# The head of a hybrid decoder step: new order of squares, normalizing products, masks and gate products

## The chip, the cores and the metric

The kernel runs on one core of a Trainium2 chip. The metric is device time in microseconds (us) for one launch; the median of the runs is compared. The core has a matrix engine (PE, which multiplies out of the on-chip memory into accumulation banks), a vector engine (DVE), an activation engine (ACT), a general engine (POOL) and a queue (SP) that issues nearly all transfers. Each engine runs its own instructions strictly in the order of its queue; semaphores order them between engines.

## The reference

One layer of a hybrid decoder on 512 prompt tokens and 8 x 8 sample tokens (576 columns in all), model width 1024:

```python
u = rmsnorm(h, norm_mix);  proj = u @ w_in            # z, xbc, dt | r, k, v, w_lo, a_lo, g_lo
prev = concat([shift_state, rw])[:, :-1]
u = rw + (prev - rw) * shift_mu                       # token shift, RWKV-7 part
w = -softplus(-(w0 + tanh(w_lo) @ w2)) - 0.5
a = sigmoid(a0 + a_lo @ a2)
gate = sigmoid(g_lo) @ g2                             # g_lo: 128 columns
# RWKV-7 recurrence, per-head group norm, bonus, output gate
# Mamba-2 SSD on conv(xbc), silu(z) gate, grouped RMSNorm
h += concat([y_ssd, y_rwkv]) @ w_out
h += swiglu(rmsnorm(h));  h += sigmoid(rmsnorm(h) @ w_plg) * (p @ w_plp);  y = rmsnorm(h)
```

Beside y the final and new states are returned.

## The kernel before

Everything is kept transposed: 128 channels on the partitions, 576 tokens along the free dimension. An input of 1024 channels is eight tiles x0 to x7. Products run in three passes, so that two reduced-precision halves stand for one full-precision number: a raw weight block (four 128x128 blocks, 256 KB) is loaded by SP, ACT rounds it to a high half `whi`, and POOL or DVE subtracts to get the low half `wlo` (`wsplit`, L197; the engine alternates through `flip` unless `only[0]` names one). `wload` (L211) takes a block that was loaded early from the list `ahead`, if there is one. Two blocks make a projected tile; `mm3` (L219) issues high x high, high x low, low x high in two column halves, 48 matrix products a tile. The result goes to one of two `lin` banks (`lin_ps`, L107).

The head, in the order of the code:

- Constants and masks (L120 to L179): `ones`, `blk`, `ident` and the masks are written by POOL; `dgmask` is multiplied by `dmb` on DVE (L164 to L167).
- The shift states `sst` are loaded (L263), then a weight block, then x0 to x7 with a second block behind x3 (L290 to L298).
- Per x tile, ACT makes the high half of x times the norm weight (L303) and DVE the low half (L304): `XU`, the input without its token-wise norm factor.
- Per x tile the square, by ACT (POOL for x3), and running sums on DVE (L307 to L317); the square tiles have four buffers in two pairs. `rstd_by_token` sums over channels on PE (L332), takes the root on ACT (L336) and the reciprocal on DVE (L337), and transposes it to all partitions (L340); ACT copies it to `r0` (L345, L346).
- `shifted` (L356) projects a tile and applies the token shift. With `early` it multiplies `XU` and scales the result by `r0` afterwards (`u`, L361), which frees the bank. ACT starts the shifted tile (L366), DVE finishes it with three operations (L368, L369, L371), ACT saves two pieces for the output.
- `norm_x` (L350) makes the normalized x on DVE (L352) and splits it in a high half (ACT) and a low half (`split`, L194; POOL and DVE in turn).
- LORA (L428) is the first projected tile, with a tanh and a split; then `norm_x(3)`, GATE (`gate_in`, L432), `norm_x(5)`.
- Then the four quarters (L926). Quarter 0 takes two of its six tiles, then the eight gate products (`gates`, L439: two weight blocks, eight times six matrix products, ACT copies each result, SP writes it out), then the other four tiles (`fill_for`). Below they are called t0 to t5, all `early`. `prep`, `gram`, `solve`, `chain` and `head_norm` follow per quarter, with further projected tiles as fillers between them.

The order of instructions in each engine's queue is not that of the code: a planner simulates the program and hands out what is ready, with the order of the code as priority. `tc.issue_after(ins)` ties the instructions of its block that run on the engine of `ins` behind `ins` in that queue.

Of the kernel before, what the change touches and what calls it, by code (L numbers as in the profile page):

```python
# [8 lines left out]
F32 = mybir.dt.float32  # L9
F32R = mybir.dt.float32r  # L10
AF = mybir.ActivationFunctionType
# [5 lines left out]
P = 128  # L17
D = 1024
NT = 576
# [56 lines left out]
def hybrid_step(ctx, tc, A):  # L76
# [15 lines left out]
    def act(out, in_, func=AF.Copy, scale=1.0, bias=0.0):  # L92
        return S.activation(out, in_, func, bias=bias, scale=scale)  # L93
# [13 lines left out]
    def lin_ps(off=224):  # L107
        return lin_bank()[:, off:off + NT]
# [19 lines left out]
    def par(name, i=0):  # L128
        at, _ = PV[name]
        return pv[:, at + i:at + i + 1]  # L130
# [30 lines left out]
    for h in range(2):  # L161
        keep(dmb[h * 64:h * 64 + 64, :], [[-8, 8]], 0, 1)
        keep(dmb[h * 64:h * 64 + 64, :], [[8, 8]], 7, -1)
    for i in range(2):  # L164
        V.tensor_tensor(dgmask[:, i, :].rearrange("p (b t) -> p b t", b=8),
                        dgmask[:, i, :].rearrange("p (b t) -> p b t", b=8),
                        dmb[:].unsqueeze(2).to_broadcast([P, 8, 8]), ALU.mult)  # L167
    hw = const("hw", [P, 76])
    at, _ = PV["w0"]
    V.tensor_scalar(hw[:, 0:16], pv[:, at:at + 16], 0.5, None, ALU.mult)  # L170
# [40 lines left out]
    def wload(nk, hi=None, lo=None):  # L211
        if ahead:
            return ahead.pop(0)
        n = nk * P
        src = A["wts"][wat[0]:wat[0] + P * n].rearrange("(p n) -> p n", p=P)
        wat[0] += P * n
        return wsplit(src, n, hi, lo)
# [42 lines left out]
    G.memset(rmask[:, 128:NT:64], 0.0)  # L260

    sst = se.tile([P, 26, 9], F32, tag="sst", name="sst")
    nc.sync.dma_start(sst[:], A["s_shift"])  # L263
    sho = se.tile([P, 26, 9], F32, tag="sho", name="sho")

    def cx_ps():
# [21 lines left out]


    xr = []  # L290
    early_w = [wload(4)]
    for k in range(KT):
        x = slot("x")
        nc.sync.dma_start(x[:], A["xT"][k])
        xr.append(x)
        if k == 3:
            early_w.append(wload(4))
    ahead += early_w  # L298
    xu = [(se, sp)[i].tile([P, KT, NT], F32R, tag=f"G{i}", name=nm("xu")) for i in range(2)]
    XU = []  # L300
    for k in range(KT):
        hi, lo = xu[0][:, k], xu[1][:, k]
        act(hi, xr[k][:], AF.Identity, scale=par("norm_mix", k))  # L303
        V.scalar_tensor_tensor(lo, xr[k][:], par("norm_mix", k), hi.bitcast(F32), ALU.mult, ALU.subtract)  # L304
        XU.append((hi, lo))
    accs = {}
    for k in range(KT):  # L307
        sq = (se, sp)[k % 2].tile([P, NT], F32, tag=f"bk{k % 2}", name=nm("sq"), bufs=2)
        e = G if k in SQP else V
        if e is G:  # L310
            G.tensor_tensor(sq[:], xr[k][:], xr[k][:], ALU.mult)
        else:
            act(sq[:], xr[k][:], AF.Square)
        if e in accs:
            e.tensor_tensor(sq[:], sq[:], accs[e][:], ALU.add)
        accs[e] = sq
    V.tensor_tensor(accs[V][:], accs[V][:], accs[G][:], ALU.add)  # L317
    r0 = sp.tile([P, NT], F32, tag="gt", name=nm("rstd"), bufs=2)
# [26 lines left out]
    act(r0[:, 0:448], banks[0][:, 0:448])  # L345
    act(r0[:, 448:NT], banks[1][:, 0:128])  # L346

    X = []

    def norm_x(n):  # L350
        for k in range(len(X), len(X) + n):
            V.scalar_tensor_tensor(xr[k][:], xr[k][:], par("norm_mix", k), r0[:], ALU.mult, ALU.mult)  # L352
            X.append(split(xr[k][:], xp, ("xhi", "xlo"), [P, NT]))


    def shifted(c, early=False, odd=False):  # L356
        ps = lin_ps()
        if early:
            linear(XU, ps)
            u = se.tile([P, NT], F32, tag="ar", name=nm("u"), bufs=2)  # L360
            V.tensor_tensor(u[:], ps, r0[:], ALU.mult)  # L361
            ps = u[:]
        else:
            linear(X, ps)
        t = sp.tile([P, NT], F32, tag="vo", name=nm("rw"), bufs=2) if odd else slot("rw")
        act(t[:], ps, AF.Identity, scale=omu[:, c:c + 1])  # L366
        mu = par("shift_mu", c)
        V.scalar_tensor_tensor(t[:, 0:65:8], sst[:, c, :], mu, t[:, 0:65:8], ALU.mult, ALU.add)  # L368
        V.scalar_tensor_tensor(t[:, ND + 1:NT], ps[:, ND:NT - 1], mu, t[:, ND + 1:NT], ALU.mult, ALU.add)  # L369
        t8, p8 = (a[:, 0:ND].rearrange("p (b t) -> p b t", b=8) for a in (t, ps))  # L370
        V.scalar_tensor_tensor(t8[:, :, 1:8], p8[:, :, 0:7], mu, t8[:, :, 1:8], ALU.mult, ALU.add)  # L371
        act(sho[:, c, 0:8], ps[:, 7:64:8])
        act(sho[:, c, 8:9], ps[:, NT - 1:NT])
        return t
# [72 lines left out]

    norm_x(3)
    ugh = gate_in()
    norm_x(5)  # L450


    H = (slice(0, 64), slice(64, 128))
# [17 lines left out]
    def fill(n=1):  # L471

        for _ in range(min(n, len(todo))):
            which, c = todo.pop(0)
            if which == "xbc":
                conved(c)
            elif which == "z":
                zed(c)
            elif which == "dt":
                dts()  # L480
            else:
                Q[which].t.append(shifted(c, which == 0, which % 2 and len(Q[which].t) > 3))
# [442 lines left out]

    for s in Q:  # L926
        if s.q == 0:
            fill(2)
            gates(ugh)
        fill_for(s)  # L930
        prep(s)
        start_states(s)
        gram(s)
        bonus(s)
        decayed(s)
        if s.q < 3:
            inverse(s)
            chain(s)
            head_norm(s)
# [733 lines left out]
```

## Time and profile before

| | us |
|---|---|
| median of 3 runs | 1346.01 |
| lowest, highest run | 1341.81, 1350.75 |
| span of the profiled execution, first to last instruction | 1349.0 |

The profiled execution has no time of its own beside its span; the span lies 3.0 us above the median of the three runs and inside their spread. An instruction's row in the order of time reads: start, duration, engine, line, operation, output<-inputs, shapes, and in brackets how long the engine had been idle before it and which instruction ended the wait. L93 is the helper through which all ACT operations go, so they are told apart by the names of their tiles. A line with a count merges neighbours.

### The profile page before, as it was taken

The numbers are of one execution on the slowest core, as the hardware profiler recorded it, in microseconds if no ns is written. First come the engines' busy times: TensorE is split into PE (matmuls) and PEld (weight loads), VectorE is DVE, ScalarE is ACT, GpSimd is POOL, SyncE is SP. The second block draws the span as 40 slices with busy tenths as digits, with TensorE's granted clock in tenths as the row PEclk, the third lists the DMA queues.
The fourth block names the chain that finished last, engine by engine and source line by source line (L and its number), as shares of the span: only waits on it lengthen the run. The fifth ranks groups of instructions, "written<-read, shape, count | busy, mean of one in ns | idle before, by whom it ended". The sixth has DMA issues, their size and how long they took to land.

```text
span 1349.0 us, 26596 instructions
## 1 busy us (share of the span) xinstructions
PE 1246.8 (92%) x10525; PEld 1150.7 (85%) x10525; DVE 826.0 (61%) x1443; ACT 618.9 (46%) x1256; POOL 625.6 (46%) x597
## 2 busy tenths in 40 slices
PE   6897999999989978899999969989999999999997
PEld 6787897889868957788779859889999999999997
DVE  6648666887687785943466667886553135443454
ACT  6565436534654463343434364464442124433363
POOL 5425413642355154122456645565654336654642
PEclk9897799899979978889989989998999999999998
DMA  5322242234232412262454542222323222314322
GB/s 164 125 68 66 77 117 63 85 103 116 75 99 78 109 41 80 94 214 83 157 176 131 179 125 72 73 93 88 92 88 87 79 86 82 93 59 149 96 89 71
DMA packets 94461, 135.58 MB, mean 100 GB/s; under 512 B 34705, under 2 KB 39057, under 8 KB 94337
## 3 DMA queue, kind: packets, MB, share of 16 engines
q1 hardware_dynamic: 93760, 133.36, 32.4%
q8 instruction: 83, 1.36, 0.4%
q10 hardware_dynamic: 576, 0.52, 0.1%
q14 instruction: 42, 0.34, 0.1%
HBM read 106.10 MB, written 27.75 MB: 99 GB/s over the span
## 4 chain that ended last, share of the span: by engine, by line
PE 63%; DVE 14%; ACT 4%; issue 4%; DMA 3%; POOL 3%; DVEq 0%; SPq 0%; ACTq 0%; POOLq 0%
PE lin L234 21%; PE lin L1403 8%; PE lin L223 6%; PE lin L221 6%; PE lin L222 6%; DVE h L395 2%; PE lin L1508 1%; PE lin L1509 1%; PE lin L1510 1%; DVE tmp L674 1%; DVE wlo L206 1%; DVE Tt L676 1%; PE lin L613 1%; PE cx L797 1%; DVE suv L831 1%
## 5 line engine op out<-in xcount | busy, mean ns | idle before, releaser
L206 POOL TENSOR_TENSOR wlo<-raw,whi 128x512 fp32r<-128x512 f32 (+1 forms) x108 | 146.4, 1356 | 352.5 <-ACT whi L93 269.5
L93 ACT ACTIVATE whi<-raw 128x512 fp32r<-128x512 f32 (+1 forms) x232 | 143.3, 618 | 259.1 <-PE lin L234 126.4
L221 PE MATMUL lin<-xhi,whi 128*128 128x288 f32 (+1 forms) x784 | 243.3, 311 | 2.5 <-ACT whi L93 2.2
L223 PE MATMUL lin<-xhi,wlo 128*128 128x288 f32 (+1 forms) x784 | 241.5, 308 | 2.3 <-POOL wlo L206 2.3
L222 PE MATMUL lin<-xlo,whi 128*128 128x288 f32 (+1 forms) x784 | 241.5, 308 | 0.3 <-POOL xlo L194 0.3
L206 DVE TENSOR_TENSOR wlo<-raw,whi 128x512 fp32r<-128x512 f32 (+1 forms) x124 | 100.9, 814 | 103.2 <-PE lin L234 60.4
L221 PEld LDWEIGHTS lin<-xhi,whi 128*128 128x128 f32 (+1 forms) x784 | 151.0, 193 | 9.3 <-ACT whi L93 2.6
L223 PEld LDWEIGHTS lin<-xhi,wlo 128*128 128x128 f32 (+1 forms) x784 | 150.7, 192 | 6.2 <-POOL wlo L206 2.8
L222 PEld LDWEIGHTS lin<-xlo,whi 128*128 128x128 f32 (+1 forms) x784 | 150.8, 192 | 4.8 <-issue 1.2
L234 PE MATMUL lin<-xhi,whi 128*128 128x288 f32 x384 | 62.3, 297 | 3.2 <-ACT xhi L93 3.0
L234 PE MATMUL lin<-xlo,whi 128*128 128x288 f32 x384 | 60.8, 298 | 0.0
L234 PE MATMUL lin<-xhi,wlo 128*128 128x288 f32 x384 | 59.3, 297 | 0.0
L234 PEld LDWEIGHTS lin<-xhi,whi 128*128 128x128 f32 x384 | 54.6, 189 | 3.8 <-ACT xhi L93 1.7
L234 PEld LDWEIGHTS lin<-xlo,whi 128*128 128x128 f32 x384 | 54.8, 191 | 0.0
L234 PE MATMUL lin<-ah,wlo 128*128 128x288 f32 x352 | 54.7, 296 | 0.0
L234 PE MATMUL lin<-al,whi 128*128 128x288 f32 x352 | 54.7, 296 | 0.0
L234 PE MATMUL lin<-ah,whi 128*128 128x288 f32 x352 | 54.7, 296 | 0.0
L234 PEld LDWEIGHTS lin<-xhi,wlo 128*128 128x128 f32 x384 | 54.3, 191 | 0.0
L1403 PE MATMUL lin<-T,wh 128*128 128x288 f32 x320 | 50.1, 296 | 4.5 <-DVE T L194 2.8
L674 DVE TENSOR_TENSOR tmp<-L,Tt 72x30 f32<-72x30 f32 (+14 forms) x120 | 49.2, 410 | 3.2
L234 PEld LDWEIGHTS lin<-ah,whi 128*128 128x128 f32 x352 | 49.6, 189 | 0.0
L234 PEld LDWEIGHTS lin<-ah,wlo 128*128 128x128 f32 x352 | 49.6, 189 | 0.0
(425 smaller groups left out, 3197.8 us busy)
## 6 DMA issues: line engine op xcount, KB each, us to landing
raw<-wts SPq DMA_DIRECT2D x271, 256.0 KB, 2.6
S<-s_wkv SPq DMA_DIRECT2D x8, 512.0 KB, 5.1
hd<-s_ssm SPq DMA_DIRECT2D x8, 512.0 KB, 4.5
o_ssm_s<-hd SPq DMA_DIRECT2D x8, 512.0 KB, 2.9
xbc_d<-E SPq DMA_DIRECT2D x12, 288.0 KB, 2.1
x<-xT SPq DMA_DIRECT2D x8, 288.0 KB
gate_d<-g SPq DMA_DIRECT2D x8, 288.0 KB, 2.5
bv_d<-rw SPq DMA_DIRECT2D x8, 288.0 KB
```

What stands on the lines that cost most here:

```text
L93: return S.activation(out, in_, func, bias=bias, scale=scale)
L206: eng.tensor_tensor(lo[:, 0:n], raw[:, 0:n], hi[:, 0:n].bitcast(F32), ALU.subtract)
L221: T.matmul(ps[:, a:b], whi, xhi[:, a:b], start=first, stop=False)
L222: T.matmul(ps[:, a:b], whi, xlo[:, a:b], start=False, stop=False)
L223: T.matmul(ps[:, a:b], wlo, xhi[:, a:b], start=False, stop=last)
L234: T.matmul(ps[:, a:e], (hi, lo)[p][:, i * P:(i + 1) * P], xs[k + i][q][:, a:e], start=n == k + i == 0, stop=n == 2 and k + i == nk - 1, sk ...
L395: V.scalar_tensor_tensor(h[:], E[:, i:i + 600], w(i), h[:], ALU.mult, ALU.add)
L613: T.matmul(ps[:, c:c + 128].rearrange("p (a t) -> p a t", a=2), s.BK[jj][H[e], g].rearrange("p a t -> p (a t)"), s.G[H[e], g, jj, :, e], s ...
L674: V.tensor_tensor(o, L[:, jx:jx + 1, jx + 1:32].to_broadcast([NB, jx, n]), Tt[:, 0:jx, jx:jx + 1].to_broadcast([NB, jx, n]), ALU.mult)
L676: V.tensor_tensor(Tt[:, 0:jx, jx + 1:32], Tt[:, 0:jx, jx + 1:32], o, ALU.subtract)
L797: T.matmul(uw[H[e], jj, :], TT[H[e], g, jj, :], xs[H[e], jj, :], start=True, stop=True)
L1403: T.matmul(ps, (hi, lo)[p][:, k * P:(k + 1) * P], OPS[n][k][q], start=first and p == q == k == 0, stop=p == 1 and k == 3, skip_group_check ...
```

## The change

Seven edits, all in the head:

1. Ten full-precision products of `ones` with itself go into a `lin` bank ahead of the first weight block. Nothing reads the bank.
2. The low half of the first weight block goes to DVE; from then on all low halves of weights go to POOL, until quarter 0 has four tiles.
3. The load of the shift states moves from ahead of the first weight block to behind x5.
4. On ACT all squares, and on DVE all their sums, are tied behind the conversions of x7.
5. The mask products on DVE move from the constants to behind the last low half of x.
6. `norm_x` is tied behind the last operation of the latest token shift on DVE, its low halves all go to DVE, and after GATE only one x tile is normalized; the other four follow one by one behind t0 to t3.
7. The gate products come after four tiles of quarter 0, not two.

```diff
-    for i in range(2):
-        V.tensor_tensor(dgmask[:, i, :].rearrange("p (b t) -> p b t", b=8),
-                        dgmask[:, i, :].rearrange("p (b t) -> p b t", b=8),
-                        dmb[:].unsqueeze(2).to_broadcast([P, 8, 8]), ALU.mult)
...
-    nc.sync.dma_start(sst[:], A["s_shift"])
...
+    t = lin_ps()
+    for _ in range(10):
+        T.matmul(t[:, 0:P], ones[:], ones[:], start=True, stop=True)
+    only[0] = V
     early_w = [wload(4)]
+    only[0] = G
     for k in range(KT):
...
+        if k == 5:
+            nc.sync.dma_start(sst[:], A["s_shift"])
...
-        act(hi, xr[k][:], AF.Identity, scale=par("norm_mix", k))
-        V.scalar_tensor_tensor(lo, xr[k][:], par("norm_mix", k), hi.bitcast(F32), ALU.mult, ALU.subtract)
+        last = (act(hi, xr[k][:], AF.Identity, scale=par("norm_mix", k)),
+                V.scalar_tensor_tensor(lo, xr[k][:], par("norm_mix", k), hi.bitcast(F32), ALU.mult, ALU.subtract))
         XU.append((hi, lo))
+    with tc.issue_after(last[1].ins):
+        for i in range(2):
+            V.tensor_tensor(dgmask[:, i, :].rearrange("p (b t) -> p b t", b=8),
+                            dgmask[:, i, :].rearrange("p (b t) -> p b t", b=8),
+                            dmb[:].unsqueeze(2).to_broadcast([P, 8, 8]), ALU.mult)
...
-            act(sq[:], xr[k][:], AF.Square)
+            with tc.issue_after(last[0].ins):
+                act(sq[:], xr[k][:], AF.Square)
         if e in accs:
-            e.tensor_tensor(sq[:], sq[:], accs[e][:], ALU.add)
+            with tc.issue_after(last[1].ins) if e is V else nullcontext():
+                e.tensor_tensor(sq[:], sq[:], accs[e][:], ALU.add)
...
-    X = []
+    X, shifts = [], []
     def norm_x(n):
         for k in range(len(X), len(X) + n):
+          with tc.issue_after(shifts[-1].ins):
             V.scalar_tensor_tensor(xr[k][:], xr[k][:], par("norm_mix", k), r0[:], ALU.mult, ALU.mult)
-            X.append(split(xr[k][:], xp, ("xhi", "xlo"), [P, NT]))
+            X.append(split(xr[k][:], xp, ("xhi", "xlo"), [P, NT], lo_eng=V))
...
-        V.scalar_tensor_tensor(t8[:, :, 1:8], p8[:, :, 0:7], mu, t8[:, :, 1:8], ALU.mult, ALU.add)
+        shifts.append(V.scalar_tensor_tensor(t8[:, :, 1:8], p8[:, :, 0:7], mu, t8[:, :, 1:8], ALU.mult, ALU.add))
...
     norm_x(3)
     ugh = gate_in()
-    norm_x(5)
+    norm_x(1)
...
         if s.q == 0:
-            fill(2)
+            for _ in range(4):
+                fill()
+                norm_x(1)
+            only[0] = None
             gates(ugh)
         fill_for(s)
```

## The prediction

> **What bounds the kernel now.** I read the page first, then the waits of PE alone in the first 90 us, then the order of PE, DVE, ACT and POOL there. The whole program is PE's:
>
> ```profile
> span 1349.0 us, 26596 instructions
> PE 1246.8 (92%) x10525; PEld 1150.7 (85%) x10525; DVE 826.0 (61%) x1443; ACT 618.9 (46%) x1256; POOL 625.6 (46%) x597
> ```
>
> PE is idle for 8% of the span, so time comes back only where PE stands still or runs at a lower clock. The change touches the head: two projected tiles (LORA, GATE), then quarter 0's six tiles t0 to t5 and eight gate products. PE's waits there:
>
> ```profile
> PE lin L221 <- ACT xu L93: 6.6, 1, 6.6
> PE lin L223 <- DVE wlo L206: 5.4, 1, 5.4
> PE lin L223 <- POOL wlo L206: 2.1, 1, 2.1
> PE lin L221 <- DVE u L361: 1.6, 1, 1.6
> ```
>
> The columns are total, times, longest, in us. 6.6 is the wait for the first input; 5.4 is a wait in t1 for a low weight half that stood in DVE's queue; 1.6 is t0 waiting for a bank that `u` has to empty, which needs the norm factor r0. PE in order of time, and under it one row of the table by stretches (its last three figures are granted clock, DMA share, GB/s):
>
> ```profile
> 27.80 0.71 PE L340 MATMUL cx<-ident,rn 128*128 128x128 f32 x5
> 30.09 0.38 PE L221 MATMUL lin<-xu,whi 128*128 128x288 f32 x1 [1.57 <-DVE u L361]
> 40.20 0.30 PE L222 MATMUL lin<-xu,whi 128*128 128x288 f32 x1
> 45.93 0.61 PE L223 MATMUL lin<-xu,wlo 128*128 128x288 f32 x1 [5.44 <-DVE wlo L206]
> 46.34 0.45 PE L221 MATMUL lin<-xu,whi 128*128 128x288 f32 x1
> 46.58 0.45 PE L222 MATMUL lin<-xu,whi 128*128 128x288 f32 x1
> 50.41 0.30 PE L223 MATMUL lin<-xu,wlo 128*128 128x288 f32 x1
> 50.95 0.29 PE L221 MATMUL lin<-vo,whi 128*128 128x288 f32 x1
> 59.31 0.30 PE L221 MATMUL lin<-xu,whi 128*128 128x288 f32 x1
> ...
> 45.00:50.00 5.00, 4.07 (x17) 4.07 (x18) 5.00 (x8) 2.13 (x5) 3.92 (x2) 0.50 0.21 59
> ```
>
> Starts are 0.24 us apart after the 5.44 us wait (46.34 to 46.58), at a granted clock of 0.50, until 50.41: the wait cost its length and then half the clock for 4 us. And DVE:
>
> ```profile
> 22.29 0.76 DVE L317 TENSOR_TENSOR sq<-sq,sq 128x576 f32<-128x576 f32 x1
> 26.11 0.19 DVE L337 RECIPROCAL rn<-rn 128x5 f32<-128x5 f32 x1 [2.46 <-ACT rn L93]
> 29.19 0.76 DVE L361 TENSOR_TENSOR u<-lin,rstd 128x576 f32<-128x576 f32 x1
> 32.72 6.68 DVE L352 SCALAR_TENSOR_TENSOR x<-x,pv,rstd 128x576 f32<-128x576 f32 x5
> 39.46 1.96 DVE L369 SCALAR_TENSOR_TENSOR rw<-u,pv,rw 128x511 f32<-128x511 f32 x1
> 43.02 0.74 DVE L369 SCALAR_TENSOR_TENSOR rw<-u,pv,rw 128x511 f32<-128x511 f32 x1
> 45.20 0.68 DVE L206 TENSOR_TENSOR wlo<-raw,whi 128x512 fp32r<-128x512 f32 x1
> 78.65 0.76 DVE L361 TENSOR_TENSOR u<-lin,rstd 128x576 f32<-128x576 f32 x1 [3.65 <-PE lin L223]
> 85.04 0.76 DVE L361 TENSOR_TENSOR u<-lin,rstd 128x576 f32<-128x576 f32 x1 [3.69 <-PE lin L223]
> ```
>
> Five normalizing products hold DVE for 6.68 us ahead of LORA's shift, and the weight half at 45.20 comes after all of it. The last two rows close t4 and t5, and DVE had been idle for over 3.6 us before each: a tile on a free PE is 85.04 - 78.65 = 6.39 us, or 0.133 for each of its 48 products.
>
> **The change part by part.** Two points frame the sum: the start of t0 (30.09) and the end of t5 (`u` at 85.04), 54.95 us apart.
>
> *From t0 to t5.* Six tiles are 6 x 6.39 = 38.3 us, the gate products 59.31 - 50.95 = 8.4 us, together 46.7. The other 8.3 us are the 5.44 us wait, the slow clock behind it and smaller waits. The change takes their cause away: only one normalizing product stays between GATE and t0, four stand behind the shifts of t0 to t3, and each sits behind the latest shift in DVE's queue; the low weight halves all go to POOL until the fourth tile. So I credit 8.3. The debit is POOL, now alone with the halves:
>
> ```profile
> 39.29 0.62 ACT L93 ACTIVATE whi<-raw 128x512 fp32r<-128x512 f32 x1
> 44.46 2.70 POOL L194 TENSOR_TENSOR ull<-rw,ulh 128x576 fp32r<-128x576 f32 x1 [3.58 <-ACT ulh L93]
> 63.32 1.29 POOL L206 TENSOR_TENSOR wlo<-raw,whi 128x512 fp32r<-128x512 f32 x1 [5.95 <-ACT whi L93]
> 39.46 1.42 POOL L194 TENSOR_TENSOR xlo<-x,xhi 128x576 fp32r<-128x576 f32 x1 [1.41 <-ACT xhi L93]
> ```
>
> A half tile of weights lasts PE 6.39 / 2 = 3.2 us; its conversion takes 0.62 on ACT and 1.29 on POOL, so 1.3 us are spare. The split of LORA (2.70) stands in the same queue: 2.70 - 1.3 = 1.4 us late, once. I take 1.5 us; the ends are 0 and another 5.4. The low halves of x move from POOL to DVE: three more operations of about 0.76 us, beside tiles in which DVE idles for 3.6 us and more; nothing, and if that cover failed, `u` has a spare tile time, since a second bank is filling. The gate products wait for the same ACT copies as now; behind t3 their input is old, which is worth some tenths, taken as 0.
>
> *Up to t0.* r0 needs the squares of all eight x tiles. ACT and the transfers:
>
> ```profile
> 5.00:10.00 5.00, 1.21 (x2) 0.57 (x2) 2.87 (x9) 4.53 (x8) 4.62 (x16) 1.00 1.00 345
> 5.80 0.78 ACT L93 ACTIVATE xu<-x,pv 128x576 fp32r<-128x576 f32 x1 [0.27 <-DMA x<-xT]
> 20.71 0.69 ACT L93 ACTIVATE sq<-x 128x576 f32<-128x576 f32 x1 [3.35 <-DVE sq L315]
> 24.51 1.28 ACT L93 ACT_TABLE_LOAD   x1
> 25.81 0.27 ACT L93 ACTIVATE rn<-cx,eps_t 128x5 f32<-128x5 f32 x1
> x<-xT SPq DMA_DIRECT2D x8, 288.0 KB
> 12.81 1.31 DVE L165 TENSOR_TENSOR dgmask<-dgmask,dmb 128x64 bf16<-128x64 bf16 x2
> ```
>
> Estimate from these rows: the first x is there at 5.8; seven more of 0.295 MB and a weight block of 0.262 MB at 345 GB/s take 6.7 us, so the last lands at 12.5. In the queue of transfers, the one of the shift states goes past a weight block and six x; the bytes ahead of the last x stay, so it lands when it did, and the first shift needs the states only after r0. The last conversion ends at 12.5 + 0.78 = 13.3, and now all squares start there: two are done at 13.3 + 2 x 0.69 = 14.7. The mask products (1.31), now behind the last low half (13.3 + 0.76 = 14.1), hold DVE to 15.4. The buffers make the rest serial, as the 3.35 us wait of a square on DVE shows: five sums at 0.76 to 19.2, a square of 0.69 to 19.9, two sums to 21.4. Before it was 22.29 + 0.76 = 23.05: 1.65 gained. GATE's weight conversions stand behind such waiting squares on ACT; a square waits for two sums, 1.5 us, about what a half tile spares (1.3), so they cost 0.2, inside GATE, whose end does not set t0.
>
> The column sums that follow:
>
> ```profile
> 24.10 0.75 PE L332 MATMUL cx<-ones,sq 128*64 128x1 f32 x20
> ```
>
> From there to `u` it took 29.19 - 23.05 = 6.1 us. Of these the column sums waited for PE to 24.10, the root for a table load (24.51 + 1.28), the transposes until 27.80, though their input was done at 26.30. Without these three waits 2.6 us are left.
>
> In the change GATE ends at about 22 (the last x half at 14.1, 0.8 us for its products, 6.4 for GATE, up to 0.8 for a cold clock): the sums come when PE has nothing else, and I take 3.0 us. So `u` is at 24.4 and t0 0.9 later, at 25.3: 4.8 us earlier. Bounds: 6.0 (no mask delay, 2.6 us), and 0.5 (all of today's waits and one collision of 1.2 us, below).
>
> *Constant products.* Ten products of constants, put ahead of all work:
>
> ```profile
> 0.95 0.21 POOL L135 MEMSET ones<- 128x128 f32 x1
> 143.72 2.13 PE L246 MATMUL lin<-lo,blk 128*128 128x288 f32 x4
> ```
>
> Four such full-precision records with 288 columns took 2.13 us; ten products of 128 columns are twenty records, 20 x 0.53 x 128/288 = 4.7 us, from 1.2 (the constants are there) to 5.9. PE's first input comes at 5.80 + 0.78 = 6.6 now, so they are covered; uncovered they would cost at most 0.4. Their gain, a faster LORA, is also bounded: LORA ends with the last x. The first low half on DVE takes away the 2.1 us wait on POOL, and for the same reason it gives nothing by itself. All: 0.
>
> *Sum.* 4.8 + 8.3 - 1.5 = 11.6 us; the profiled span 1349.0 becomes 1337.4. That execution is 3.0 above the median of the three runs (1346.01), and the head holds nothing that varies so much, so I take the gain from the median: 1334.4, stated as 1334. All behind t5 hangs on its tiles and moves with it.
>
> **The rivals.**
>
> *The wait comes back elsewhere.* The shift at 39.46 took 1.96 us beside a POOL operation of 1.42, the one at 43.02 only 0.74: 1.2 us for one collision. [...] Eleven weight halves on POOL give eleven chances; where ACT's next conversion stands behind a stretched DVE operation, PE waits again. One wait of 5.4 us and the 1.8 us of clock behind it (17 products, 0.24 against 0.13) in place of my 1.5 leave 5.9 us: 1340. For it: ACT and DVE stay strictly in order. Against: PE's weights no longer stand in DVE's queue. Chance 0.2.
>
> *The clock falls ahead of t0.* GATE done at 22, t0 at 25.3: PE has 3.3 us with only sums and transposes. 1.57 us idle left the clock up in this trace, 5.44 dropped it. If it drops, t0 starts with 1.8 us of loss: 1336. [...] Chance 0.1.
>
> *All waits go.* 6.0 ahead of t0, 8.3, and the gate products at their bare 6.4 us (2.0 less): 16.3 us, 1330. For it: DVE was idle in most of t2 to t5. Against: the gates' copies on ACT. Chance 0.2.
>
> *Slower.* The planner orders each engine by its own simulated times, so an earlier head shifts what it puts between the serial steps of quarter 0's solve. One such filler on the chain:
>
> ```profile
> 128.03 1.86 DVE h L395
> ```
>
> Seven more of 1.86 us in the chain eat 11.6 us, from there it is slower; fourteen give 1334.4 + 26.0 = 1360, and eight 1349. For it: such fillers stand on the chain of waits now. Against: as much can leave it. Chance 0.1, half of it over 1%.
>
> **How the numbers follow.** The forecast has 0.4 (1331 to 1338), and its faster third passes 1%. Over 1% is about what a measurement of this kernel can tell from no change: 13.5 us, 1332.5. Faster: 0.2 + 0.13 = 0.33; slower: 0.05; same: the other 0.62. The range takes in all waits gone with some of the planner's luck (1326) and the wait that comes back with some of its bad luck (1344).
>
> **What would show it.** Right: no PE wait over 2 us between t0 and t5, 0.13 us spacing throughout, t0 at 24 to 26, `u` of t5 at 72 to 75, DVE's normalizing products one by one behind shifts. Wrong: t0 later than 28 (the squares' serial chain was under-sized), a wait on POOL's low halves of more than 3 us, 0.24 us spacing in t0, or a t5 that ends early while the span does not follow.

## The result and the profile after

| | before | after |
|---|---|---|
| median of 7 runs each, side by side, us | 1347.94 | 1358.63 |
| lowest, highest, us | 1339.56, 1350.75 | 1354.25, 1361.41 |
| span of the profiled execution, us | 1349.0 | 1355.5 |
| mean granted clock of that execution | 0.940 | 0.932 |
| start of t0, us | 30.09 | 29.78 |
| `u` of t5, us | 85.04 | 83.07 |

The ratio is 1.0098, with a 95% interval of 1.007 to 1.0126: slower, outside the range and on the other side of the forecast. Two executions further down, one of e6 (5668 us) and one of e9 (6334 us), were slow beyond all others and are left out of the ratios. The two last rows of the table split the miss. The head was to end 11.6 us earlier and ends 2.0 us earlier. And what lies behind the head did not move with it: it lost some 13 us more than that.

The page of the changed kernel opens like this (busy us, share of the span, instructions):

```profile
span 1355.5 us, 26638 instructions
PE 1259.5 (93%) x10545; PEld 1160.7 (86%) x10545; DVE 829.5 (61%) x1441; ACT 619.7 (46%) x1256; POOL 628.4 (46%) x599
```

PE is busy for 12.7 us more than before (1246.8) and does the same work but for the 4.64 us of constant products. So part of the loss is not idle time but matrix products at a lower granted clock (0.932 for 0.940 over the execution). The waits of PE alone in the first 90 us, in total, times and longest:

```profile
PE lin L219 <- POOL wlo L202: 4.1, 2, 2.7
PE lin L217 <- DVE u L371: 1.4, 1, 1.4
PE cx L341 <- DVE sq L326: 1.2, 1, 1.2
```

The 5.4 us wait on a low half from DVE is gone. Two waits on low halves from POOL have come in its place, 1.49 us in LORA and 2.66 us in t1. In order of time on PE, and under it two rows of the table by stretches (busy us of PE, PEld, DVE, ACT and POOL, granted clock, DMA share, GB/s):

```profile
1.21 4.64 PE L288 MATMUL lin<-ones 128*128 128x128 f32 x20 [1.21 <-POOL ones L135]
13.45 0.61 PE L219 MATMUL lin<-xu,wlo 128*128 128x288 f32 x1 [1.49 <-POOL wlo L202]
17.68 0.29 PE L218 MATMUL lin<-xu,whi 128*128 128x288 f32 x1
25.73 0.75 PE L341 MATMUL cx<-ones,sq 128*64 128x1 f32 x20 [1.24 <-DVE sq L326]
29.78 0.61 PE L217 MATMUL lin<-xu,whi 128*128 128x288 f32 x1 [1.38 <-DVE u L371]
41.15 0.61 PE L219 MATMUL lin<-xu,wlo 128*128 128x288 f32 x1 [2.66 <-POOL wlo L202]
...
24.00:28.00 4.00, 2.16 (x29) 1.84 (x27) 1.84 (x2) 2.18 (x3) 2.71 (x2) 0.88 0.32 72
28.00:32.00 4.00, 2.62 (x11) 2.22 (x10) 2.85 (x6) 2.82 (x9) 0.00 (x0) 0.50 0.20 61
```

GATE ends at 25.73 - 1.24 = 24.49, the column sums wait for the last sum of squares, and t0 begins at half the clock: its first product takes 0.61 us instead of 0.38. ACT, then DVE:

```profile
13.07 1.81 ACT L93 ACTIVATE sq<-x 128x576 f32<-128x576 f32 x3
18.06 0.63 ACT L93 ACTIVATE whi<-raw 128x512 fp32r<-128x512 f32 x1 [2.65 <-POOL wlo L202]
18.59 1.25 ACT L93 ACTIVATE sq<-x 128x576 f32<-128x576 f32 x2
20.71 0.69 ACT L93 ACTIVATE sq<-x 128x576 f32<-128x576 f32 x1 [0.87 <-DVE sq L324]
22.44 0.69 ACT L93 ACTIVATE sq<-x 128x576 f32<-128x576 f32 x1 [1.04 <-DVE sq L324]
```

```profile
12.45 3.18 DVE L306 SCALAR_TENSOR_TENSOR xu<-x,pv,xu 128x576 fp32r<-128x576 f32 x2 [0.18 <-ACT xu L93]
15.83 2.70 DVE L324 TENSOR_TENSOR sq<-sq,sq 128x576 f32<-128x576 f32 x2
19.30 3.11 DVE L324 TENSOR_TENSOR sq<-sq,sq 128x576 f32<-128x576 f32 x3 [0.76 <-ACT sq L93]
23.16 0.76 DVE L324 TENSOR_TENSOR sq<-sq,sq 128x576 f32<-128x576 f32 x1 [0.75 <-ACT sq L93]
24.02 1.65 DVE L326 TENSOR_TENSOR sq<-sq,sq 128x576 f32<-128x576 f32 x1
28.97 1.42 DVE L371 TENSOR_TENSOR u<-lin,rstd 128x576 f32<-128x576 f32 x2 [1.95 <-ACT rstd L93]
34.75 0.82 DVE L362 SCALAR_TENSOR_TENSOR x<-x,pv,rstd 128x576 f32<-128x576 f32 x1
35.48 2.09 DVE L190 TENSOR_TENSOR xlo<-x,xhi 128x576 fp32r<-128x576 f32 x3
37.48 0.46 DVE L445 TENSOR_SCALAR rw<-rw 128x576 f32<-128x576 f32 x1
37.86 0.76 DVE L190 TENSOR_TENSOR xlo<-x,xhi 128x576 fp32r<-128x576 f32 x1
83.07 0.76 DVE L371 TENSOR_TENSOR u<-lin,rstd 128x576 f32<-128x576 f32 x1 [3.66 <-PE lin L219]
```

The squares do start at 13.07, as forecast. But behind three of them a conversion of GATE's weights stands in ACT's queue that waits 2.65 us, and the four squares left for ACT stand behind it. Its row names POOL, whose half had ended at 15.78 + 1.27 = 17.05, a microsecond earlier. The conversion writes one of two `whi` buffers, and the last product of LORA that reads this one ends at 17.68 + 0.29 = 17.97: what it waited for is LORA, which is late by the 1.49 us wait at 13.45 and a granted clock of 0.50 from 13.4 to 16.8. Of the seven sums on DVE four take 0.76 us each; the three that begin while POOL is in a subtraction (the first, the third and the last) take 1.84, 1.38 and 1.65. The last sum ends at 24.02 + 1.65 = 25.67. From there to `u` it is 28.97 - 25.67 = 3.3 us. POOL, beside the first two sums and at the time of the 2.66 us wait:

```profile
15.78 1.27 POOL L202 TENSOR_TENSOR wlo<-raw,whi 128x512 fp32r<-128x512 f32 x1
34.94 4.94 POOL L190 TENSOR_TENSOR ull<-rw,ulh 128x576 fp32r<-128x576 f32 x1 [8.14 <-PE lin L218]
39.84 2.50 POOL L202 TENSOR_TENSOR wlo<-raw,whi 128x512 fp32r<-128x512 f32 x2
```

The split of LORA took 4.94 us where it took 2.70 before, and the first of the two low halves that t1 waits for begins only then.

Behind the head all five queues have the order of before until about 240 us, POOL and SP until about 300. From there on the planner has ordered each of them differently, with the same instructions.

### The profile page after: what moved, and what is told of

It is laid out like the page before. It is cut to its first block, busy times and chain, and to the rows that moved or that the text cites. A ratio compares the mean times of both kernels' runs of the same rounds, so it can differ in the third digit from the quotient of the medians.

```text
span 1355.5 us, 26638 instructions
## 1 busy us (share of the span) xinstructions
PE 1259.5 (93%) x10545; PEld 1160.7 (86%) x10545; DVE 829.5 (61%) x1441; ACT 619.7 (46%) x1256; POOL 628.4 (46%) x599
## 4 chain that ended last, share of the span: by engine, by line
PE 47%; DVE 5%; DMA 2%; ACT 1%; issue 1%; POOL 1%; DVEq 0%; POOLq 0%; ACTq 0%; SPq 0%
PE lin L230 22%; PE lin L1416 8%; PE lin L217 2%; PE lin L219 2%; PE lin L218 2%; PE lin L1521 1%; PE lin L1522 1%; PE lin L1523 1%; DMA hd<-sz_d 1%; PE y L1217 1%; PE d L1178 1%; DVE wlo L202 1%; PE d L1166 0%; DMA yl<-yr_d 0%; DVE xlo L1316 0%
## 5 line engine op out<-in xcount | busy, mean ns | idle before, releaser
L202 POOL TENSOR_TENSOR wlo<-raw,whi 128x512 fp32r<-128x512 f32 (+1 forms) x113 | 151.7, 1343 | 343.3 <-ACT whi L93 274.6
L202 DVE TENSOR_TENSOR wlo<-raw,whi 128x512 fp32r<-128x512 f32 (+2 forms) x119 | 99.6, 837 | 101.1 <-PE lin L230 60.7
L686 DVE TENSOR_TENSOR Tt<-Tt,tmp 72x30 f32<-72x30 f32 (+14 forms) x120 | 50.3, 419 | 3.3
L1416 PEld LDWEIGHTS lin<-T,wh 128*128 128x128 f32 x320 | 45.1, 188 | 6.5 <-DVE T L190 2.2
```

What stands on the lines that cost most here:

```text
L202: eng.tensor_tensor(lo[:, 0:n], raw[:, 0:n], hi[:, 0:n].bitcast(F32), ALU.subtract)
L686: V.tensor_tensor(Tt[:, 0:jx, jx + 1:32], Tt[:, 0:jx, jx + 1:32], o, ALU.subtract)
L1416: T.matmul(ps, (hi, lo)[p][:, k * P:(k + 1) * P], OPS[n][k][q], start=first and p == q == k == 0, stop=p == 1 and k == 3, skip_group_check ...
```

## The experiments

Fourteen kernels. Most of them hold a recorded order: a list of the traced instructions, engine by engine, from quarter 0's `prep` to about 870 us, is tied one behind the other, so that the planner is free in the head and behind 870 us and has no choice between. The ties add no instruction.

```diff
+def follow(tc):
...
+    ins = list(tc.nc.cur_bb.bb.instructions)[TAIL[-1]:]
+    for steps in json.loads(zlib.decompress(base64.b85decode(PLAN))).values():
+        at, last = 0, None
+        for d in steps:
+            at += d
+            if last is not None:
+                tc.add_manual_dep(ins[at], ins[last].name,
+                                  mybir.DependencyInfo(mybir.DependencyClass.NoSync, mybir.DependencyReason.DATA),
+                                  reason="follow")
+            last = at
...
             hybrid_step(ctx, tc, A)
+            follow(tc)
```

The results together. The ratio is to the kernel before, run beside it (its medians there were 1343.06 to 1343.85); t0 and t5 are from the profiled execution, one for each kernel.

| run | head | order behind it | ratio, 95% | start of t0 | `u` of t5 |
|---|---|---|---|---|---|
| e1 | changed | before's | 1.000 (0.998 to 1.002) | 29.89 | 81.95 |
| e2 | before's | changed kernel's | 1.0097 (1.0068 to 1.0127) | 30.18 | 85.20 |
| e3 | before's and edit 1 | planned, as before's to 870 us | 1.0022 (1.0005 to 1.0038) | 30.02 | 85.43 |
| e4 | changed without edit 1 | planned | 1.0091 (1.0059 to 1.0122) | 28.91 | 83.56 |
| e5 | changed | changed, 498 to 600 before's | 1.005 (1.0025 to 1.0075) | 30.26 | 83.88 |
| e6 | before's | before's, 500 to 592 changed | 1.0045 (1.0019 to 1.007) | 29.97 | 85.34 |
| e7 | changed without edit 4 | before's | 0.9985 (0.996 to 1.0009) | 31.48 | 84.27 |
| e8 | before's and edits 6, 7 | before's | 0.9965 (0.9943 to 0.9987) | 30.46 | 80.13 |
| e9 | changed | changed, 645 to 870 before's | 1.008 (1.005 to 1.0109) | 29.77 | 82.92 |
| e10 | changed, halves shared | before's | 0.9951 (0.9926 to 0.9976) | 28.88 | 78.54 |
| e11 | as e8 | planned | 0.9999 (0.9974 to 1.0024) | 30.01 | 79.53 |
| e12 | changed, halves shared, without edits 1, 4 | before's | 0.994 (0.9914 to 0.9965) | 28.78 | 78.48 |
| e13 | changed | before's from 498 on | 1.000 (0.9981 to 1.0019) | 29.74 | 81.83 |
| e14 | before's | changed from 500 on | 1.0087 (1.0059 to 1.0115) | 30.07 | 85.33 |

### Head or order

e1 is the changed kernel with the order of before, e2 the kernel before with the order of the changed one; the diff is the one above, with one or the other list. The second theory of e1 speaks of the clock's windows. In the trace of the changed kernel the granted clock stands at 0.50 or 1.00 for 3.41 us or a multiple of it at a time: from 13.39 us on for 3.41 us at 0.50, 10.24 at 1.00, 6.83 at 0.50, 6.83 at 1.00, 3.41 at 0.50 and 54.6 at 1.00.

> The changed kernel, but from quarter 0's prep to the feed-forward stage (about 870 us) every engine's queue is held to the order that the kernel before has there. Theory P (the loss behind 200 us is the new order that the planner gave to the rest): the head's gain of 2 to 3 us survives, so 1342 to 1347, ratio 0.996 to 1.000. Theory C (the order does not matter, the shift of 2 to 3 us against the clock's windows does): like the changed kernel, 1354 to 1361, ratio about 1.01.

> The kernel before, but from quarter 0's prep to about 870 us every queue is held to the order of the changed kernel. P: slower than before by the whole loss, 1356 to 1362, ratio 1.007 to 1.011. C: like before, ratio 0.998 to 1.002.

1343.24 and 1355.44 us, beside 1343.38 of the kernel before. With the order of before the whole loss is gone; with the old head and the new order the whole loss is there. So the order behind the head is the loss, and a head that ends at another time, or meets the clock in another phase, is not.

### The constant products

e3 is the kernel before with the ten products alone, e4 the changed kernel without them.

```diff
+    t = lin_ps()
+    for _ in range(10):
+        T.matmul(t[:, 0:P], ones[:], ones[:], start=True, stop=True)
```

> The kernel before with only the ten constant products. They take one more bank from the rotation, and that turns which of the later bank pairs the feed-forward stage uses for which product; its queues differ from before only from about 870 us on. If that turn costs, ratio 1.002 to 1.005 with all of it behind 870 us; if not, 0.999 to 1.001. The first 100 us gain at most 1 us, since LORA still ends with the last x.

> The changed kernel without the constant products. If the products do nothing but warm the clock, LORA is a few us later and t0 stays near 29.8 us, since the squares' chain sets r0: ratio to before 1.008 to 1.011. If the bank turn is part of the loss, 2 to 5 us less than the changed kernel: ratio 1.003 to 1.007. Its order behind 200 us is the planner's own and differs from before too.

1344.8 and 1352.8 us. Alone they cost 0.2%, at the edge of what the runs tell; taking them out leaves the changed kernel slow (1.0091). What e4's expectation calls warming the clock shows in part of the traces: LORA's early products start mostly 0.13 us apart in the changed kernel and e13 (from 7.4 and 7.2 us on) and 0.24 apart in e12, which has no constant products (7.99 to 10.63), but 0.24 apart too from about 9 to 12 us in e1, e7 and e10, which have them. The products are no part of the loss to speak of, and no part of a gain: without them t0 starts at 28.91, 0.9 us earlier, in one execution each. Whether their 0.2% sits behind 870 us can't be read: the traced execution of e3 took only 1341.31 us.

### Where the order loses

e5 and e6 exchange the order in one stretch of about 100 us, which holds the same instructions in both. The list is the kernel's own, with the instructions of the stretch sorted as in the other kernel; nothing but the list differs.

> The changed kernel with its own order of every queue, except in one stretch (about 498 to 600 us of its profile: the last recurrence steps of the third quarter beside the preparation and the solve of the fourth), where the instructions of that stretch stand in the order that the kernel before gives them. Theory L, the loss sits in that stretch, where recurrence steps are queued behind preparations: DVE's start times there stop slipping (they lose about 12 us against the old order), and the time falls by about 10 us to 1345. Rival D, the loss is spread over the program and the stretch only shows where the engines meet again: it falls by 3 us at most, 1352 or more.

> The reverse: the kernel before, head and all, with its own order of every queue, except in the same stretch (about 500 to 592 us of its profile), where the instructions of the stretch stand in the changed kernel's order. Theory L: about 10 us more than before, 1353, with a granted clock of 0.6 at 500 to 520 us and the state product on POOL some 4 us later behind two others. Rival D: 3 us more at most, 1346.

1349.77 and 1353.95 us, ratios 1.005 and 1.0045. Both ways round the stretch is worth about half of the loss on average. That is between the two theories: less than the 10 us of one, more than the 3 us of the other. The average hides two groups. Of e6's executions three took 1344.83 to 1346.84 us, no more than before, and six 1351.7 to 1356.33; of e5's, nine took 1346.43 to 1350.59 and three 1356.33 to 1360.77. e9 does the same with the stretch from 645 to 870 us.

> The changed kernel with its own order of every queue, except in a later stretch (about 645 to 870 us of its profile), where the instructions stand in the order of the kernel before. The stretch at 498 to 600 us gave back about half of the loss (1.005 in place of 1.0098). Theory T, two stretches carry the loss, and this one the other half: ratio about 1.005 again, 1350, and DVE's start times lose nothing more behind 645 us against the old order. Rival: the orders differ without price there, and the rest was the chance of clock and waits all along: the ratio stays at 1.008 or more.

1355.83 us, 1.008: the later stretch alone gives back little, as the rival said. e13 and e14 then take everything behind 498 us at once.

> The changed kernel with its own order up to about 498 us and the order of the kernel before from there to about 870 us of its profile, in every queue. Theory R, all of the loss arises behind 498 us, partly at 498 to 600 and the rest only where both stretches are in the new order: ratio 0.998 to 1.002, 1343. Rival U, about half of the loss comes from the order at 200 to 498 us, through the phase in which the later stretches meet the clock and the waits: ratio 1.004 to 1.006, as with the one stretch.

> The reverse: the kernel before with its own order up to about 500 us and the changed kernel's order from there to about 872 us. Theory R: 1.008 to 1.010, 1354 to 1357. Rival U: 1.004 to 1.006 as with the one stretch, 1350.

1344.06 and 1355.31 us. Up to 498 us the new order costs nothing; behind it lies all of the loss. The parts don't add: by the ratios the first stretch alone gives back half, the second alone a fifth or nothing, both together all.

The changed kernel and e13 have the same order up to 498 us, so a comparison of start times shows where the price is paid. The start times of the same DVE instructions (same tiles, same turn), changed kernel less e13, as the median over 30 us of e13 each, worked out from the two traces:

| stretch, us | 450 | 510 | 570 | 600 | 690 | 720 | 810 | 870 | 930 to the end |
|---|---|---|---|---|---|---|---|---|---|
| difference, us | 4.0 | 10.8 | 13.1 | 13.7 | 16.5 | 17.3 | 15.3 | 13.4 | 13.4 |

The 4.0 were there from 210 us on, with one and the same order: a difference from one execution to the next. Behind 498 us 6.8 us are lost at once, 2.9 more up to 600, 3.6 more up to 720, and 3.9 come back behind that. e5 has the old order up to 600 us: against e13 its start times differ by 0.1 us at 540 to 630, by 5.4 at 720 and by 6.6 from 810 on. Behind an early first stretch the new order from 600 us on costs 6.5 us; behind the late one of the changed kernel it costs 13.4 - 13.7 = -0.3. So the later stretch hides its loss behind that of the first, and gives back nothing alone.

What happens at 500 us, first in the changed kernel, then in e13: rows of POOL, PE and DVE, and two or three rows of the table by stretches.

```profile
506.55 2.87 POOL L595 TENSOR_TENSOR bk<-lo,lo 64x576 f32<-64x576 f32 x2 [0.69 <-DVE lo L591]
509.50 2.56 POOL L862 TENSOR_TENSOR S<-S,pc 128x512 f32<-128x512 f32 x2
...
515.46 2.08 PE L623 MATMUL lin<-G,bk 64*128 64x128 f32 x16 [0.23 <-DVE G L641]
518.99 1.40 PE L744 MATMUL cb<-G,S 64*64 64x16 f32 x22
523.90 1.46 PE L744 MATMUL cb<-G,S 64*64 64x16 f32 x22
525.29 1.22 PE L623 MATMUL lin<-G,bk 64*128 64x128 f32 x8
528.02 1.95 PE L623 MATMUL lin<-G,bk 64*128 64x128 f32 x22
...
532.77 0.43 DVE L633 TENSOR_TENSOR Lst<-lin,gmask 64x256 f32<-64x256 f32 x1 [0.44 <-ACT G L93]
539.34 0.69 DVE L677 TENSOR_SCALAR Tt<-L 72x1024 f32<-72x1024 f32 x1 [2.43 <-DMA L<-Ld]
...
510.00:514.00 4.00, 2.93 (x44) 2.33 (x44) 3.34 (x9) 2.36 (x8) 3.65 (x6) 1.00 0.51 190
514.00:518.00 4.00, 3.49 (x22) 2.66 (x22) 2.02 (x6) 1.03 (x4) 0.58 (x1) 0.64 0.45 152
518.00:522.00 4.00, 4.00 (x53) 3.49 (x52) 1.33 (x4) 1.41 (x4) 1.33 (x2) 0.50 0.00 0
```

```profile
501.83 1.55 POOL L862 TENSOR_TENSOR S<-S,pc 128x512 f32<-128x512 f32 x1
503.34 2.87 POOL L595 TENSOR_TENSOR bk<-lo,lo 64x576 f32<-64x576 f32 x2
506.29 1.04 POOL L862 TENSOR_TENSOR S<-S,pc 128x512 f32<-128x512 f32 x1
...
511.64 1.16 PE L623 MATMUL lin<-G,bk 64*128 64x128 f32 x16
513.84 1.60 PE L744 MATMUL cb<-G,S 64*64 64x16 f32 x48 [0.22 <-DMA S<-s_wkv]
516.32 1.16 PE L623 MATMUL lin<-G,bk 64*128 64x128 f32 x16
518.08 1.16 PE L623 MATMUL lin<-G,bk 64*128 64x128 f32 x16
...
522.00 0.43 DVE L633 TENSOR_TENSOR Lst<-lin,gmask 64x256 f32<-64x256 f32 x1 [0.45 <-ACT G L93]
528.61 0.69 DVE L677 TENSOR_SCALAR Tt<-L 72x1024 f32<-72x1024 f32 x1 [2.96 <-DMA L<-Ld]
...
510.00:514.00 4.00, 3.74 (x60) 3.06 (x56) 2.70 (x8) 2.09 (x8) 1.60 (x3) 1.00 0.40 131
514.00:518.00 4.00, 4.00 (x112) 3.85 (x110) 2.46 (x6) 1.72 (x7) 1.91 (x4) 1.00 0.02 6
```

Of each time difference 4.0 us are those of the two executions. The order on POOL is the visible mark: the fourth quarter's `bk` (L595) stands ahead of both products of the third quarter's state `S` (L862), where the first `S` came first. But it isn't the price: the second `S` ends at 512.06 and 507.33, 0.7 us later than the 4.0. The expectations of e5 and e6 had taken the mark for the cause.

The price is on PE. `lin<-G,bk` are the fourth quarter's gram products, sixteen to a batch, whose masked copies `Lst` go out by DMA and come back as the matrix `L` of its solve. In e13 a batch takes 1.16 us. In the changed kernel PE has only 2.93 of 4 us of work from 510 to 514, the granted clock is 0.64 over the next stretch and then 0.50, a batch takes 2.08 us, and the products of the sample states (`cb<-G,S`) hold PE from 518.99 to 525.4 where they took 2.6 us. Two batches stand behind them in PE's queue, in both kernels. The batch ahead of them starts 515.46 - 511.64 = 3.8 us later, no more than the two executions differ; the one behind them 525.29 - 516.32 = 9.0. The last `Lst` is written at 532.77 and not at 522.00, and the solve starts 539.34 - 528.61 = 10.7 us later, 6.7 of them from here. No projected tile runs on PE from 473 to 535 us (469 to 525 in e13), so that PE has nothing to fill the gaps with.

The other traces bear the drop out. Between 505 and 530 us the clock fell to 0.50 in five of the six traced executions with the new order there (for 13.7 us in the changed kernel and in e9, 20.5 in e2, 10.2 in e14, 3.4 in e4), and in one of nine with the old (6.8 us, in the kernel before, at 518).

The order doesn't force the drop. The trace of e6, an execution of 1344.83 us, kept a granted clock of 1.00 from 500 to 540 us in the new order, and belongs to the faster of its two groups. What decides between them is open. Nor was it tried which change of place in the stretch is the decisive one: 324 instructions on PE, 133 on DVE, 54 on ACT, and 7 or 8 each on POOL and SP stand elsewhere.

### The head's terms, with the order held

e7 takes edit 4 back, in the changed kernel with the order of before.

```diff
-            with tc.issue_after(last[0].ins):
-                act(sq[:], xr[k][:], AF.Square)
+            act(sq[:], xr[k][:], AF.Square)
...
-            with tc.issue_after(last[1].ins) if e is V else nullcontext():
-                e.tensor_tensor(sq[:], sq[:], accs[e][:], ALU.add)
+            e.tensor_tensor(sq[:], sq[:], accs[e][:], ALU.add)
```

> The changed kernel without the ties of the squares and their sums (edit 4 alone undone), every queue behind the head held to the order of the kernel before, as in the first experiment. Theory S, the ties made the squares and sums serial behind the last conversion, and GATE's weight conversions stand between them on ACT: the last sum ends at 22 to 23 rather than 25.7, t0 starts at 26.5 to 28 rather than 29.9, u of t5 falls by about 2 us to 80, and the time by 2 to 1341, less than a measurement can tell. Rival: the last sum is late for want of DVE and POOL whatever the ties, t0 stays at 29 to 30.

The last sum of squares ends at 22.12 in its trace, as both this expectation and the prediction would have it, and t0 still starts at 31.48: PE waits 3.59 us at 16.49 for one of POOL's low halves, GATE comes later for it, and in PE's queue the column sums stand behind the first half of GATE, the transposes behind all of it. Neither theory had that. Sums and GATE are two chains of about equal length, and t0 waits for both.

e8 is the kernel before with the ties of the normalizing products and the place of the gate products alone.

```diff
+          with tc.issue_after(shifts[-1].ins):
             V.scalar_tensor_tensor(xr[k][:], xr[k][:], par("norm_mix", k), r0[:], ALU.mult, ALU.mult)
-            X.append(split(xr[k][:], xp, ("xhi", "xlo"), [P, NT]))
+            X.append(split(xr[k][:], xp, ("xhi", "xlo"), [P, NT], lo_eng=V))
...
-    norm_x(5)
+    norm_x(1)
...
-            fill(2)
+            for _ in range(4):
+                fill()
+                norm_x(1)
             gates(ugh)
```

> The kernel before with only edit 6 (normalizing products and their low halves tied behind the token shifts) and edit 7 (gate products behind four tiles), the low halves of the weights still shared by POOL and DVE, and every queue behind the head held to the order of the kernel before. Theory N, the normalizing products were the whole cause of the 5.4 us wait and the low halves on POOL alone brought another wait back: t0 at 30, no wait over 2 us up to t5, 46.7 + 0.9 us from t0 to u of t5, so u of t5 at 78 and the time about 6 us below the kernel before, 1337. Rival: a wait of 2 to 3 us on a low half stays whichever engine makes it, u of t5 at 81 to 82, time 1341.

1340.67 us, and no wait over 2 us from t0 to t5: 80.13 - 30.46 = 49.7 us, 2.1 over the 47.6 expected. e10 is the changed kernel with one line of edit 2 undone.

```diff
     only[0] = V
     early_w = [wload(4)]
-    only[0] = G
+    only[0] = None
```

> The changed kernel whose low halves of weights are shared again by POOL and DVE after the first (half of edit 2 undone), every queue behind the head held to the order of the kernel before. Theory H, the low halves on POOL alone, behind a split of LORA that DVE's operations stretch to 4.9 us, make the 2.7 to 3.1 us wait at 41 us: no wait over 2 us between t0 and u of t5, u of t5 at 79 (82 with POOL alone), time 2 to 3 us under the first experiment's, 1340 to 1341. Rival: a low half queued on DVE behind a shift waits as long, u of t5 stays at 81 to 82.

1338.4 us. `u` of t5 comes 3.4 us earlier than in e1, 1.0 of them ahead of t0, and the 3.1 us wait of e1 is gone; the low halves on POOL alone were that wait. LORA's split lasts 5.57 us here, no less than in the changed kernel. But t1's first low half now comes from DVE, and for the second, behind the split on POOL, PE waits only 0.13 us.

e11 is e8 with no order held; its diff is e8's alone.

> The kernel of the last batch with edits 6 and 7 alone, but with every queue ordered by the planner itself, no order held. Its head ends 4.9 us earlier than before. Theory P, a head that ends at another time gives another order behind it, and that order is worth more than the head: the time leaves the 1340 of the held order by several us, to either side, most likely up to 1345 to 1355. Rival: a gain in the head is kept, 1339 to 1342, and the changed kernel's loss was its own.

1343.63 us, between the two theories' ranges. The head's gain is there (`u` of t5 at 79.53), and the time isn't: between the ratios of e8 and e11 lie 0.0034, some 4.6 us, with intervals that overlap. Against e3, whose order is that of before, its DVE start times stand at -7.4 us at 480, -3.9 at 600, and between -0.4 and 0.6 from 1020 on.

e12 takes edits 1 and 4 and that half of edit 2 out of the changed kernel and holds the order of before.

> The changed kernel without the constant products, without the ties of the squares and with the low halves shared after the first one (edits 1 and 4 and half of edit 2 undone; the moves of the shift states and the masks, the ties of the normalizing products and the place of the gate products stay), every queue behind the head held to the order of the kernel before. If these three edits were what cost the head its gain: t0 at 28 to 29, u of t5 at 76 to 78, 1337 to 1339. If the last sum of squares is late for other reasons: t0 at 30, u of t5 at 80, 1340 as with the ties and gates alone.

1335.27 us beside 1343.06, ratio 0.994: faster than both kernels. PE and DVE, and the stretch in which t0 starts:

```profile
25.10 0.75 PE L336 MATMUL cx<-ones,sq 128*64 128x1 f32 x20
28.78 0.37 PE L217 MATMUL lin<-xu,whi 128*128 128x288 f32 x1 [1.58 <-DVE u L366]
...
78.48 0.76 DVE L366 TENSOR_TENSOR u<-lin,rstd 128x576 f32<-128x576 f32 x1 [3.69 <-PE lin L219]
...
24.00:28.00 4.00, 3.20 (x37) 2.54 (x36) 1.01 (x3) 1.87 (x5) 0.33 (x1) 1.00 0.23 66
28.00:32.00 4.00, 3.22 (x24) 3.25 (x25) 3.82 (x8) 3.19 (x8) 0.00 (x0) 1.00 0.22 68
```

The column sums follow GATE's products without a wait, PE stands still only for the 1.58 us just ahead of t0, and the clock stays at 1.00. The five runs with the order of before line up: ends of t5 at 84.27, 81.95, 80.13, 78.54 and 78.48 go with 0.9985, 1.000, 0.9965, 0.9951 and 0.994. Neighbours in this list can't be told apart, its ends can. With the order held a head that ends 6.5 us earlier than before's 85.04 is worth 6.6 (0.0049 x 1343) to 8.1 us.

## Why the prediction was wrong

**The step that failed** is the last of the sum: "All behind t5 hangs on its tiles and moves with it." It holds for the instructions, not for their order. With the order held the rest did follow the head, within what the runs tell (e1, e8, e10, e12); with the planner free a head that ends 2.0 us earlier cost 10.7 us, and of the 22.3 us between the forecast change (-11.6) and the measured one (+10.7) the order is 12.7. e2 measures it without the new head: 12.1. The other 9.6 us are the head: 4.5 up to t0 and 5.1 from t0 to t5.

**The rival "Slower"** had the right cause, the planner's choices, and the wrong place and chance. It looked at fillers in quarter 0's solve; the price lies behind 498 us, where the third quarter's recurrence and the fourth's gram products share a PE that has no projected tile at that time, and the traces show it paid in clock. "As much can leave it" was the argument for 0.1. The two orders tried here that the planner made for a new head lost 12 us in the changed kernel and, less surely, some 5 in e11. Two cases don't make a rule, but the chance of 0.05 for slower by 1% was argued from nothing that the trace could show.

**Up to t0: 4.8 forecast, 0.3 found.** The squares start when forecast and the tail from the last sum to `u` is 3.3 us (3.0 forecast). Mis-sized was the end of the sums, 25.67 for 21.4, and most of it is DVE beside POOL, which the sum up to t0 held at no cost and its lower bound at one collision. The last low half of x ended at 12.45 + 3.18 = 15.63 for 14.1. The seven sums, counted at 0.76 each or 5.3 us, lasted 2.70 + 3.11 + 0.76 + 1.65 = 8.2. The idle time between them, 1.6 us for 0.7, is the smaller part. I had put a waiting GATE conversion at 0.2 us, "inside GATE, whose end does not set t0"; the one at 18.06 held ACT for 2.65 us, but in e1, with the same head, it held ACT for 1.22 us and the last sum still ended at 25.63. That the first low half on DVE "takes away the 2.1 us wait on POOL" failed too: 1.49 us of it came back at LORA's second block. And e7 shows that GATE's end can set t0: with the sums done at 22.12, GATE sets t0. In no trace did t0 start ahead of 28.78. The upper bound of 6.0 was out of reach, because "GATE ends at about 22" was. Its 0.8 us for a cold clock was an estimate with no row beside it; in the changed kernel the clock was at 0.50 from 13.39 to 16.80 us, and twelve products of LORA started 0.24 us apart (13.85 to 16.73) where 0.13 is the spacing at 1.00, which is 1.3 us.

**The rival "The clock falls ahead of t0"** came true beside the rest: 0.50 in 28 to 32 us. The trace's clock records have it fall at 27.0 us; in the 3.4 us before, PE was busy for 1.64 us and no gap exceeded 1.24 us. So it took no long stretch without work: thin work was enough to lose the clock. In e12, with GATE still running, it stayed up (3.20 of 4 us).

**From t0 to t5: 8.3 - 1.5 = 6.8 forecast, 54.95 - 53.29 = 1.7 found.** The cause of the credit was right and its size 3.0 too high: e8, e10 and e12 take 49.7 us, 5.3 gained of 8.3. The debit was mis-sized: against e10, whose t0 starts at half the clock as well, it is 53.29 - 49.66 = 3.6 for 1.5. POOL's split of LORA was put at 2.70 us and took 4.94, and PE's wait behind it cost the clock again (0.50 from 40.7 to 44.1 us). The rival "The wait comes back elsewhere" named this wait, and priced one collision at 1.2 us. In the trace DVE has no gap from 34.75 to 38.6, six instructions one behind the other, and the split ends at 34.94 + 4.94 = 39.88, which is 1.42, the length of such a subtraction at 39.46 in the kernel before, behind 38.46: it fits a split that was held off by the whole train. In five traces (before, changed, e8, e10, e12) this split ends 1.35 to 1.38 us after the start of the `u` behind the train, whose product it reads from a bank, though it began 1.3 to 4.2 us ahead of that `u`; the 2.70 us of the kernel before were such a wait already. So one collision was too small a unit: in these traces the split lasted 2.70 to 5.57 us, the longer the earlier it began ahead of that `u`.

**Constant products: 0 forecast.** Right in the head, where they end ahead of the first input (1.21 + 4.64 = 5.85; 5.9 forecast). e3's 0.2% is as small as a measurement of this kernel can tell. That they also take one turn of the `lin` banks, and that the planner then orders the feed-forward stage differently, was not in the prediction.

**The normalizing products** went one by one behind shifts, and no weight half waited on DVE, as said; e8 shows that this edit with the place of the gate products helps, 0.9965 with the order held.

## What to carry to other kernels

Where a planner that simulates the program orders the queues, an edit near the start is two edits: itself, and a new order for everything behind it. Hold the old order when the edit is measured, and then keep the order that is better; here the same head was worth 0.9965 with one order and 0.9999 with the other, though with intervals that overlap, and in e1 and the changed kernel 1.000 and 1.0098, with intervals that don't. Before a chain is credited with an earlier end, add up the other chain that the same consumer waits for, and count an operation of POOL against the whole train of DVE operations that it can meet, not against one (here a split of 2.70 us became one of 4.94), and the DVE operations as longer where POOL runs beside them (here sums of 0.76 us took 1.38 to 1.84).

## What the runs showed of the hardware that was not expected

- With one order of the queues the start times of e5 and e13, two kernels, stayed within 0.2 us of each other from 210 to 630 us. Between other executions whole offsets came in at single places: the changed kernel and e13 differ by 1.3 us at 120, 2.6 at 150, and 3.9 to 4.0 from 210 to 480 us with one order.
- A POOL subtraction of 128x576 lasted 1.42 and 2.70 us in the kernel before, 4.94 in the changed one and 5.57 in e10, with different trains of DVE operations beside it.
- In the changed kernel the granted clock fell to 0.50 at 27.0 us though PE was busy for 1.64 of the 3.4 us before and had no gap over 1.24 us, and at 515.1 us though it was busy for 2.07 of 3.4 us and had no gap over 0.71. The share alone doesn't tell: from 504.9 to 508.3 us PE was busy for 54% and the clock stayed at 1.00.
